# A recurrent layer in a new order: remainders on VectorE, gelu-branch tiles between the gate groups and through DRAM, and a fixed order of the last products

## Chip, cores and metric

The kernel runs on one core of one Trainium2 chip. The metric is the device time in microseconds of one execution. Several executions are timed and their median counts; one execution is profiled, and all rows below come from it.

## What is computed

A decoder trunk of two layers over 1024 tokens of width 1024, in float32. The change touches the mixer of the first layer, the start of both SwiGLU stages, and the final norm:

```python
def rglru_mixer(h, w_in, conv_w, conv_b, w_ra, b_ra, w_ix, b_ix, lam, w_out):
    u = h @ w_in
    xb, yb = u[..., :D_RNN], u[..., D_RNN:]          # D_RNN = 1536
    y = jax.nn.gelu(yb)
    xc = causal_conv4(xb, conv_w) + conv_b
    r = sigmoid(block_diag(xc, w_ra) + b_ra)          # 16 blocks of 96
    i = sigmoid(block_diag(xc, w_ix) + b_ix)
    log_a = -8.0 * r * softplus(-lam)
    a = exp(log_a)
    bx = sqrt(-expm1(2 * log_a)) * (i * xc)
    rec = scan(lambda h, (a, b): a * h + b, a, bx)    # over the tokens
    return (rec * y) @ w_out

h = x + rglru_mixer(rmsnorm(h), ...)
h = h + swiglu(rmsnorm(h), w_gu[0], w_down[0])
h = h + nsa_mixer(rmsnorm(h), shared_kv)
h = h + swiglu(rmsnorm(h), w_gu[1], w_down[1])
return rmsnorm(h) * final_g
```

## The kernel before

Activations lie transposed, channels on the 128 partitions and the 1024 tokens along the row. Every float32 product is done by three matmuls of rounded parts (`mm3`): each operand is split (`split`) into a rounded part, the hi part, copied by ScalarE, and the remainder, the lo part, which is the operand less its hi part, on VectorE or, with `pool=True`, on GpSimd. There are 49 SBUF slots of 128x1024 and 8 PSUM banks of 128x512; a tile gets a slot when an earlier one has been read for the last time. A scheduler sets each engine's order from modelled durations, except where a `manual_schedule` block keeps the order of the program: in `rglru` that holds for ScalarE, VectorE and SyncE until `man.close()`.

**Recurrent layer** (`rglru`). w_in gives 12 x tiles and 12 y tiles of 128 channels, 48 matmuls of 128x512 each. An x tile is evicted from PSUM with the norm's row factor rb (tile xb, L390), convolved on ScalarE and in three VectorE steps (xc, L396), and split into ch and cl; its last 32 partitions go by DMA into the tiles c3h and c3l, as the 16 blocks of 96 channels lie across tiles (`chain`). Every three x tiles have one gate group (`gates`): 16 PSUM tiles pg (48 matmuls), a sigmoid of each on ScalarE (tiles ra and ix, L424), and six DMAs that bring the last 32 partitions back. The group's elementwise work (`ew`) then follows in four steps spread over the next tiles as the table `EW` says: tanh, exp and square root on ScalarE (t, e, s), on VectorE ix times xc (m, L446) and per tile one r step: v (L451), times v (L452) and the scan over the tokens (L453), whose result goes to DRAM (rec, L455). A y tile is evicted (y, L496 or L510), kept in SBUF, and at the end put through gelu, multiplied by the reloaded rec (recl) and split into zh and zl, with which the product with w_out begins (po). TensorE's order before is x0 x1 x2 x3 x4 y0 g0 x5 x6 x7 y1 g1 x8 x9 x10 y2 g2 x11 y3 y4 y5 g3 y6 y7 and then, outside the manual block, y8 to y11.

The weights are loaded ahead and split in the order of their use by `wpump`; the splits numbered 4 to 21 (`WPOOL`) have their remainder on GpSimd, as has every cl.

**FFN stages**, each cut into products numbered i. While the first run, the row factor of the norm is made: sums (pms), a root (`rstd_a`, on VectorE with one power on GpSimd) giving two diagonal tiles dg (L298), and four matmuls prb (L310, `rstd_b`) that spread it over the partitions, after product i = 6.

**Tail.** The last product of the down projection (pU, then pW in two halves of 256 tokens) is added to h; sums of squares of the finished columns run on ScalarE, VectorE and GpSimd; `finish` makes root, dg (L288), prb (L1086) and 16 or 8 output multiplications (out, L1092) for one part of the tokens: 512, then 256, then 256, each sent to DRAM from SyncE or ScalarE.

Of the kernel before, what the change touches and what calls it, by code (L numbers as in the profile page):

```python
# [7 lines left out]
F32 = mybir.dt.float32  # L8
# [5 lines left out]
P = 128  # L14
# [16 lines left out]
GATE_T = [4, 7, 10]  # L31
EW = "t e m0,s m1 m2 r0,r1 r2"
WPOOL = (4, 22)
# [12 lines left out]
XA = 3  # L46

# [20 lines left out]
class Trunk:  # L68
# [44 lines left out]
    def weights(self):  # L113
        d = self.d
        w = []
        def gate_w(g):
            w.append((f"ra{g}", d["w_ra"][g], 384))
            w.append((f"ix{g}", d["w_ix"][g], 384))

        for t in range(DRNN_T):  # L120
            w.append((f"x{t}", d["w_in"][t], 1024))
            if t in GATE_T:
                g = GATE_T.index(t)
                w.append((f"y{g}", d["w_in"][12 + g], 1024))
                gate_w(g)
        for t in range(3, DRNN_T):
            w.append((f"y{t}", d["w_in"][12 + t], 1024))
            if t == 5:
                gate_w(3)
# [73 lines left out]
    def wpump_(self, nload, nsplit):  # L203
# [12 lines left out]
        while self.wsplit < min(nsplit, cap):  # L216
# [8 lines left out]
            self.split(hi[:r, :n], lo[:r, :n], raw[:r, :n], WPOOL[0] <= self.wsplit < WPOOL[1])  # L225
# [44 lines left out]
    def rstd_a(self, ss, nb=KD):  # L270
# [43 lines left out]
    def rglru(self):  # L314
# [72 lines left out]
        def chain(t):  # L387
# [12 lines left out]
            self.split(hi, lo, xc, True)  # L400
# [4 lines left out]
            for a, b in zip(st["x3"], (hi, lo)):  # L405
                nc.sync.dma_start(a[32 * j:32 * j + 32, :].bitcast(F32), b[96:128, :].bitcast(F32))
# [3 lines left out]
        def gates(g, mid=()):  # L410
# [3 lines left out]
            for nme, dst, cb in (("ra", rr, C_BRA), ("ix", ii, C_BIX)):  # L414
                whi, wlo = self.wget(f"{nme}{g}")
# [13 lines left out]
                for b in range(3):  # L429
                    nc.sync.dma_start(dst[b][96:128, :], o[32 * b:32 * b + 32, :])  # L430
# [17 lines left out]

            def scan(b):
                t = 3 * g + b  # L450
                nc.vector.scalar_tensor_tensor(vv[b], rr[b], 1.0, vv[b], op0=ALU.add, op1=ALU.mult)  # L451
                nc.vector.tensor_tensor(ii[b], ii[b], vv[b], ALU.mult)  # L452
# [6 lines left out]
            for b in range(3):  # L459
                fs[f"m{b}"] = lambda b=b: mul(b)  # L460
                fs[f"r{b}"] = lambda b=b: scan(b)
# [16 lines left out]
        def yload(t):  # L478
            if t < DRNN_T:
                recs[t] = self.slot("recl")  # L480
                nc.gpsimd.dma_start(recs[t], st[("rec", t)])
# [1501 lines left out]
```

## Time and profile before

| | |
|---|---|
| runs | 2738.09, 2741.74, 2742.91 us; median 2741.74 |
| the profiled execution | 2742.32 us, span 2740.6 us, mean granted TensorE clock 0.988 |
| busy: TensorE, VectorE, ScalarE, GpSimd | 97%, 69%, 47%, 41% of the span |
| recurrent layer up to the first po | 0 to 346.4 us |
| FFN stage 0 begins, FFN stage 1 begins | 477 us, 2067 us |

Times in the rows are microseconds from the start of the span unless marked ns. In a timeline a row gives start, duration, engine, program line, operation, output from inputs, shape, and in brackets the idle time of the engine just before it with what ended it. L followed by a number is a line of the kernel before.

### The profile page before, as it was taken

How to read it: one execution, taken by the hardware profiler on the slowest of the kernel's cores; microseconds unless marked ns; L12 is line 12 of the kernel's file. 1: busy time of each engine (PE TensorE's matmuls, PEld its weight loads, DVE VectorE, ACT ScalarE, POOL GpSimd, SP SyncE). 2: the span in 40 equal slices, each digit the busy share in tenths (PEclk: the TensorE clock that was granted, in tenths of full speed). 3: DMA queues.
4: the chain of work that ended last, by engine and by line, in shares of the span. 5: the costliest groups of instructions: out<-in, count | busy, mean ns of one | idle time of the engine just before them, and what ended most of it. 6: DMA issues, size and time to landing. Idle time of an engine off the chain costs nothing.

```text
span 2740.6 us, 36687 instructions
## 1 busy us (share of the span) xinstructions
PE 2658.2 (97%) x12650; PEld 2204.7 (80%) x12650; DVE 1892.1 (69%) x3641; ACT 1301.7 (47%) x2505; POOL 1120.5 (41%) x1102
## 2 busy tenths in 40 slices
PE   8989999999999999999999999999999999999997
PEld 6867888788888778888888878888887888887786
DVE  8655734755555898647647999999856545557997
ACT  4656622433223443424415888989934323223433
POOL 2431103444333555110004677777634434436552
PEclk9998999999999999999999999999999999999998
DMA  3323533466564975353485322221354666559761
GB/s 126 93 83 104 170 143 111 112 156 166 150 161 117 324 201 112 133 154 91 162 244 155 82 67 59 67 76 49 108 174 104 170 156 152 154 128 287 194 146 62
DMA packets 175178, 377.03 MB, mean 138 GB/s; under 512 B 16896, under 2 KB 66432, under 8 KB 174992
## 3 DMA queue, kind: packets, MB, share of 16 engines
q1 hardware_dynamic: 121232, 256.79, 28.8%
q0 software_dynamic: 51872, 115.43, 19.6%
q10 hardware_dynamic: 1888, 2.46, 0.2%
q8 instruction: 100, 1.64, 0.2%
q14 instruction: 86, 0.70, 0.1%
HBM read 289.68 MB, written 78.64 MB: 134 GB/s over the span
## 4 chain that ended last, share of the span: by engine, by line
PE 68%; DVE 13%; issue 4%; DMA 3%; ACT 2%; POOL 1%; POOLq 0%; DVEq 0%; SPq 0%; ACTq 0%
PE pb L777 13%; PE pc L777 8%; PE pa L777 8%; PE pn L239 7%; PE pU L1022 6%; PE psc L239 4%; PE po L239 4%; DVE so L232 3%; PE pt L1644 2%; PE py L239 2%; PE pV L1022 2%; PE pwo L1834 2%; PE pW L1022 1%; PE po L1682 1%; PE po L1683 1%
## 5 line engine op out<-in xcount | busy, mean ns | idle before, releaser
L232 DVE TENSOR_TENSOR so<-wr,so 128x512 fp32r<-128x512 f32 (+1 forms) x476 | 390.9, 851 | 55.2 <-ACT so L231 54.6
L231 ACT ACTIVATE so<-wr 128x512 fp32r<-128x512 f32 (+1 forms) x476 | 279.1, 611 | 247.1 <-DMA wr<-w_dn 114.3
L777 PE MATMUL pb<-so,so 128*128 128x512 f32 x1584 | 382.8, 392 | 0.7 <-DVE so L232 0.7
L777 PEld LDWEIGHTS pb<-so,so 128*128 128x128 f32 x1584 | 300.2, 190 | 63.6 <-DVE so L232 1.1
L777 PE MATMUL pa<-so,so 128*128 128x512 f32 x1056 | 254.2, 393 | 4.1 <-ACT ev L786 2.6
L777 PE MATMUL pc<-so,so 128*128 128x512 f32 x1056 | 255.6, 389 | 0.0
L190 POOL DMA_DIRECT2D wr<-w_gu x176 | 161.6, 1076 | 226.0 <-DVE so L232 178.9
L1022 PE MATMUL pU<-so,so 128*128 128x512 f32 x1056 | 245.4, 390 | 2.3 <-DVE so L232 2.3
L777 PEld LDWEIGHTS pa<-so,so 128*128 128x128 f32 x1056 | 199.5, 189 | 46.6 <-DVE so L232 2.7
L239 PE MATMUL psc<-kl,ql 96*128 96x512 f32 (+2 forms) x960 | 232.8, 368 | 2.1 <-DVE thl L232 1.2
L1022 PEld LDWEIGHTS pU<-so,so 128*128 128x128 f32 x1056 | 197.9, 188 | 45.3 <-DVE so L232 4.0
L777 PEld LDWEIGHTS pc<-so,so 128*128 128x128 f32 x1056 | 198.3, 188 | 41.1
L805 ACT ACTIVATE ev<-ev 128x512 f32<-128x512 f32 x44 | 27.8, 632 | 349.4 <-POOL ev L804 349.4
L239 PEld LDWEIGHTS psc<-kl,ql 96*128 96x128 f32 x960 | 164.1, 190 | 24.7 <-PE pt L1644 2.2
L190 POOL DMA_DIRECT2D wr<-w_dn x96 | 91.4, 1136 | 135.7 <-DVE so L232 46.1
L804 POOL TENSOR_TENSOR ev<-ev,rb 128x512 f32<-128x512 f32 x44 | 58.2, 1322 | 209.0 <-DVE ev L803 209.0
L232 DVE TENSOR_TENSOR wl<-wr,wh 128x1024 fp32r<-128x1024 f32 (+4 forms) x79 | 87.8, 1127 | 77.5 <-ACT wh L231 53.2
L232 DVE TENSOR_TENSOR thl<-pt,thl 128x512 fp32r<-128x512 f32 x198 | 133.0, 681 | 10.3 <-ACT thl L231 10.1
L1022 PE MATMUL pV<-so,so 128*128 128x512 f32 x528 | 125.0, 392 | 8.6 <-DVE so L232 6.0
L231 ACT ACTIVATE wh<-wr 128x1024 fp32r<-128x1024 f32 (+4 forms) x97 | 90.1, 956 | 77.6 <-DMA wr<-w_q 19.7
L1022 PEld LDWEIGHTS pV<-so,so 128*128 128x128 f32 x528 | 98.2, 188 | 33.4 <-DVE so L232 7.7
L231 ACT ACTIVATE thl<-pt 128x512 fp32r<-128x512 f32 x198 | 114.5, 597 | 20.2 <-PE pt L1644 18.8
(331 smaller groups left out, 6366.7 us busy)
## 6 DMA issues: line engine op xcount, KB each, us to landing
wr<-w_gu SPq DMA_DIRECT2D x110, 512.0 KB, 4.8
wr<-w_gu POOLq DMA_DIRECT2D x176, 256.0 KB, 5.1
zd<-ev SPq DMA_DIRECT2D x44, 512.0 KB, 3.2
zr<-zd SPq DMA_DIRECT2D x44, 512.0 KB, 6.3
wr<-w_dn SPq DMA_DIRECT2D x40, 512.0 KB, 7.2
wr<-w_dn POOLq DMA_DIRECT2D x64, 256.0 KB, 5.1
ql<-qd SPq DMA_DIRECT2D x64, 192.0 KB, 3.1
wr<-w_in SPq DMA_DIRECT2D x23, 512.0 KB, 3.8
```

The costliest lines, as they stand in the source:

```text
L190: self.nc.gpsimd.dma_start(dst, src, accum_op=ALU.add)
L231: nc.scalar.activation(hi, src, AF.Copy)
L232: (nc.gpsimd if pool else nc.vector).tensor_tensor(lo, src, hi.bitcast(F32), ALU.subtract)
L239: self.nc.tensor.matmul(ps, a, b, start=j == 0, stop=j == n - 1)
L777: nc.tensor.matmul(p, a, b, start=k + n == 0 and j in (1, 5, 6), stop=k == 3 and n == 2, skip_group_check=j not in (1, 5, 6))
L804: nc.gpsimd.tensor_tensor(t0[:, hi], t0[:, hi], rb[:, hi], ALU.mult)
L805: nc.scalar.activation(t0[:, hi], t0[:, hi], AF.Silu)
L1022: nc.tensor.matmul(ps, a, b, start=k + n == 0 and j in (1, 5, 2), stop=k == G[g] - 1 and n == 2, skip_group_check=j not in (1, 5, 2))
L1644: nc.tensor.transpose(pt[:, h * P:(h + 1) * P], Pt[n][h][r][:, off:off + P], self.ident)
L1682: nc.tensor.matmul(po[n], v, thl[:, 0:512], start=False, stop=False)
L1683: nc.tensor.matmul(po[n], v, thl[:, 512:1024], start=False, stop=end)
L1834: self.nc.tensor.matmul(p, wk[a], x[b], start=k + j == 0, stop=k == KD - 1 and j == 2)
```

## The change

**Recurrent layer.** The table `RG` gives one order of x tiles, y tiles and gate groups (g): TensorE now runs x0 x1 x2 y0 x3 x4 y1 g0 x5 x6 y2 x7 g1 x8 y3 x9 x10 y4 g2 x11 y5 y6 g3 y7 y8 and then y9 y10 y11. All remainders are VectorE's. A group's weights are one 768-wide tile. The small moves (c3h, c3l, ra, ix) go to GpSimd's DMA queue. The elementwise work is cut finer (a: L451 of before, b: L452, c: the scan) and all of it is issued before the next gates. Every y tile is stored to DRAM after its eviction and loaded again with rec, two tiles ahead of its use; gelu, product and split of a z follow each other.

**FFN stages.** The four prb matmuls come after product i = 7 and ahead of i = 8; two pairs of small operations of the root are one each.

**Tail.** The remainders for the last product are made earlier; the order of TensorE, VectorE, ScalarE and GpSimd from the last product on is written out (`tail`): 24 pW matmuls ahead of prb, the first quarter's root beside the second quarter's products, tiles 4 to 7 scaled by ScalarE and multiplied by GpSimd, output in smaller pieces.

```diff
-GATE_T = [4, 7, 10]
-EW = "t e m0,s m1 m2 r0,r1 r2"
-WPOOL = (4, 22)
+RG = "y0 x3 x4 y1 g0 x5 x6 y2 x7 g1 x8 y3 x9 x10 y4 g2 x11 y5 y6 g3 y7 y8"
+EW = "t e m0 s m1 m2 a0 b0,c0 a1 b1 c1,a2 b2,c2"
...
-            self.split(hi[:r, :n], lo[:r, :n], raw[:r, :n], WPOOL[0] <= self.wsplit < WPOOL[1])
+            self.split(hi[:r, :n], lo[:r, :n], raw[:r, :n])
...
-        nc.vector.tensor_tensor(t, y, y, ALU.mult)
+        nc.vector.scalar_tensor_tensor(t, y, -0.5, y, op0=ALU.mult, op1=ALU.mult)
         nc.vector.tensor_tensor(t, t, v, ALU.mult)
-        nc.vector.tensor_scalar(t, t, -0.5, 1.5, op0=ALU.mult, op1=ALU.add)
-        nc.vector.tensor_tensor(rt, y, t, ALU.mult)
+        nc.vector.scalar_tensor_tensor(rt, t, 1.5, y, op0=ALU.add, op1=ALU.mult)
...
-            self.split(hi, lo, xc, True)
+            self.split(hi, lo, xc)
...
-                nc.sync.dma_start(a[32 * j:32 * j + 32, :].bitcast(F32), b[96:128, :].bitcast(F32))
+                nc.gpsimd.dma_start(a[32 * j:32 * j + 32, :].bitcast(F32), b[96:128, :].bitcast(F32))
...
-                    nc.sync.dma_start(dst[b][96:128, :], o[32 * b:32 * b + 32, :])
+                    nc.gpsimd.dma_start(dst[b][96:128, :], o[32 * b:32 * b + 32, :])
...
+        def yev(t, pp):
+            y = self.slot("y")
+            for p, c0 in zip(pp, (0, 512)):
+                nc.vector.tensor_tensor(y[:, c0:c0 + 512], p, st["rb"][:, c0:c0 + 512], ALU.mult)
+            dr = st[("y", t)] = self.dram(f"y{t}", [P, S])
+            nc.gpsimd.dma_start(dr, y)
             yield
+        def yload(t):
+            if t < DRNN_T:
+                recs[t] = self.slot("recl"), self.slot("yl")
+                nc.gpsimd.dma_start(recs[t][0], st[("rec", t)])
+                nc.gpsimd.dma_start(recs[t][1], st[("y", t)])
+        def z(t):
+            yload(t + 2)
+            r, y = recs.pop(t)
+            nc.scalar.activation(y, y, AF.Gelu_apprx_tanh)
+            nc.vector.tensor_tensor(y, y, r, ALU.mult)
+            hi, lo = self.slot("zh", F32R), self.slot("zl", F32R)
+            self.split(hi, lo, y)
+            zs[t] = (hi, lo)
...
+        for x in RG.split():
+            i = int(x[1:])
+            if x[0] == "g":
+                while st.get("ew"):
+                    run(ew())
+                gates(i, pend)
+                pend = iter(())
+                continue
...
-            if i == 6:
+            if i == 8:
                 st["rb"] = self.rstd_b(dg)
...
+                if (j, p) == (4, 3):
+                    with self.tc.manual_schedule(engines={getattr(mybir.EngineType, x) for x in TMS.split()}):
+                        self.tail(h, pr, fin, st, scale)
...
+        for p in range(4):
+            next(pr)
+            square(0, p)
...
+        dg = root(sums(0), side)
+        add(1, 2)
+        next(pr)
+        square(1, 3)
+        spread(0, dg)
+        for m in (4, 7, 0):
+            part(0, m)
+        dg = root(sums(1), lambda: part(0, 1))
+        for m in (5, 6, 2, 3):
+            part(0, m)
+        send(0, 4, 4, nc.sync)
+        send(0, 0, 4, nc.sync)
+        spread(1, dg)
+        for m in (4, 0, 5, 1, 6, 2, 3, 7):
+            part(1, m)
```

VectorE ahead of the third gate group (g2), before. ix, v and ra are the second group's elementwise tiles, xb and xc the x tiles 9 and 10:

```order
L453 SCALAR_TENSOR_TENSOR ix_1132<-ra_1071,ix_1132 128x1024
L396 SCALAR_TENSOR_TENSOR xc_1382<-xb_1379,cv,xc_1382 128x1023
L396 SCALAR_TENSOR_TENSOR xc_1382<-xb_1379,cv,xc_1382 128x1022
L396 SCALAR_TENSOR_TENSOR xc_1382<-xb_1379,cv,xc_1382 128x1021
L451 SCALAR_TENSOR_TENSOR v_1179<-ra_1087,v_1179 128x1024
L452 TENSOR_TENSOR ix_1152<-ix_1152,v_1179 128x1024
L453 SCALAR_TENSOR_TENSOR ix_1152<-ra_1087,ix_1152 128x1024
L390 TENSOR_TENSOR xb_1489<-px_1329,rb_386 128x512
```

VectorE ahead of the same group, in the changed kernel (x tiles 9 and 10, then y4; wl and cl are remainders):

```order
L452 SCALAR_TENSOR_TENSOR ix_1206<-ra_1150,ix_1206 128x1024
L390 SCALAR_TENSOR_TENSOR xc_1505<-xb_1502,cv,xc_1505 128x1023
L227 TENSOR_TENSOR cl_1514<-xc_1505,ch_1513 128x1024
L227 TENSOR_TENSOR wl_1525<-wr_1383,wh_1524 128x1024
L384 TENSOR_TENSOR xb_1578<-px_1452,rb_386 128x512
L390 SCALAR_TENSOR_TENSOR xc_1581<-xb_1578,cv,xc_1581 128x1023
L227 TENSOR_TENSOR cl_1587<-xc_1581,ch_1586 128x1024
L227 TENSOR_TENSOR wl_1595<-wr_1446,wh_1594 128x1024
L489 TENSOR_TENSOR y_1620<-py_1528,rb_386 128x512
```

The group's last scan (ix_1206) stood directly ahead of the eviction of x10 that frees banks for the gates (ix_1152 ahead of xb_1489); now it stands ahead of x9's convolution, with x10's eviction and chain and y4's eviction behind it, and the remainders cl and wl are rows of VectorE.

GpSimd around the second gate group, before (remainders among the stores of rec):

```order
L232 TENSOR_TENSOR cl_905<-xc_895,ch_904 128x1024
L232 TENSOR_TENSOR wl_919<-wr_773,wh_918 128x384
L455 DMA rec_914<-ix_714 128x1024
L455 DMA rec_980<-ix_725 128x1024
L232 TENSOR_TENSOR cl_991<-xc_975,ch_990 128x1024
L455 DMA rec_988<-ix_745 128x1024
L232 TENSOR_TENSOR wl_1001<-wr_836,wh_1000 128x1024
```

and in the changed kernel:

```order
L454 DMA rec_963<-ix_781 128x1024
L400 DMA c3h_648<-ch_969 32x1024
L400 DMA c3l_649<-cl_970 32x1024
L454 DMA rec_977<-ix_792 128x1024
L491 DMA y_1112<-y_1109 128x1024
L454 DMA rec_1115<-ix_803 128x1024
L425 DMA ra_1123<-ra_1161 32x1024
L425 DMA ra_1134<-ra_1161 32x1024
```

GpSimd has no arithmetic left there, and its queue holds the stores of rec and y and the small moves, each behind the ones above it.

TensorE at the start of the first FFN stage, before (pb_3454 and pb_3498 are the banks of products 6 and 7, then 8 and 9):

```order
L777 MATMUL pb_3454<-so_3297,so_3300 128x512 x3
L310 MATMUL prb_3468<-dg_3416,onesr 128x512
L310 MATMUL prb_3472<-dg_3416,onesr 128x512
L777 MATMUL pb_3498<-so_3285,so_3317 128x512 x3
L777 MATMUL pb_3498<-so_3289,so_3317 128x512 x3
L310 MATMUL prb_3468<-dg_3418,onesr 128x512
L310 MATMUL prb_3472<-dg_3418,onesr 128x512
L777 MATMUL pb_3454<-so_3363,so_3346 128x512 x3
```

and in the changed kernel:

```order
L740 MATMUL pb_3509<-so_3316,so_3344 128x512 x3
L740 MATMUL pb_3509<-so_3320,so_3344 128x512 x3
L740 MATMUL pb_3509<-so_3324,so_3344 128x512 x3
L304 MATMUL prb_3540<-dg_3442,onesr 128x512
L304 MATMUL prb_3544<-dg_3442,onesr 128x512
L304 MATMUL prb_3540<-dg_3444,onesr 128x512
L304 MATMUL prb_3544<-dg_3444,onesr 128x512
L740 MATMUL pb_3480<-so_3390,so_3373 128x512 x3
```

The twelve matmuls of the next product, which stood between the two pairs of prb, now stand ahead of all four.

## Rows read from the trace of the kernel before

**Rows 1.** The page, busy time, share of the span and instructions of TensorE:

```profile
PE 2658.2 (97%) x12650; PEld 2204.7 (80%) x12650; DVE 1892.1 (69%) x3641; ACT 1301.7 (47%) x2505; POOL 1120.5 (41%) x1102
```

**Rows 2.** Windows of the four gate groups: busy by engine, then PEclk, DMA share, GB/s:

```profile
82.31:93.69 11.38, 11.35 (x49) 7.71 (x48) 6.40 (x7) 10.42 (x16) 5.15 (x3) 1.00 0.42 127
137.26:154.91 17.65, 14.48 (x49) 9.21 (x48) 10.16 (x8) 12.65 (x19) 10.41 (x6) 0.81 0.42 131
198.48:220.68 22.20, 13.98 (x50) 9.12 (x48) 15.23 (x11) 13.34 (x18) 8.58 (x4) 0.77 0.38 122
264.25:281.09 16.84, 14.44 (x49) 9.58 (x48) 11.27 (x11) 14.16 (x19) 1.06 (x2) 0.80 0.38 120
```

**Rows 3.** Waits of TensorE, 0 to 350 us: total, times, longest:

```profile
PE pg L239 <- ACT ra L424: 11.0, 3, 8.2
```

**Rows 4.** Timeline of the third gate group, 194 to 214 us, four engines:

```profile
209.65 0.74 PE L239 MATMUL pg<-ch,wh 96*96 96x512 f32 x1 [8.22 <-ACT ra L424]
...
207.61 1.28 ACT L424 ACT_TABLE_LOAD   x1 [3.76 <-DVE ix L453]
...
194.69 2.29 DVE L453 TENSOR_TENSOR_SCAN ix<-ra,ix 128x1024 f32<-128x1024 f32 x1
...
203.22 4.32 DVE L453 TENSOR_TENSOR_SCAN ix<-ra,ix 128x1024 f32<-128x1024 f32 x1
...
202.05 3.34 POOL L232 TENSOR_TENSOR cl<-xc,ch 128x1024 fp32r<-128x1024 f32 x1 [4.24 <-ACT ch L231]
```

**Rows 5.** Groups of GpSimd, 0 to 350 us: busy us, mean ns:

```profile
L232 POOL TENSOR_TENSOR cl<-xc,ch 128x1024 fp32r<-128x1024 f32 x12 | 33.4, 2780 | 91.3 <-ACT ch L231 91.3
L232 POOL TENSOR_TENSOR wl<-wr,wh 128x1024 fp32r<-128x1024 f32 x12 | 32.0, 2680 | 43.7 <-ACT wh L231 43.6
```

**Rows 6.** Groups of VectorE, 0 to 360 us:

```profile
L453 DVE TENSOR_TENSOR_SCAN ix<-ra,ix 128x1024 f32<-128x1024 f32 x12 | 31.6, 2633 | 0.3
...
L396 DVE SCALAR_TENSOR_TENSOR xc<-xb,cv,xc 128x1023 f32<-128x1023 f32 x12 | 16.0, 1336 | 23.0 <-ACT xc L393 22.8
...
L390 DVE TENSOR_TENSOR xb<-px,rb 128x512 f32<-128x512 f32 x24 | 15.3, 682 | 30.5 <-POOL wl L232 11.6 <-PE py L239 5.4 <-DMA rec<-ix 5.2
...
L232 DVE TENSOR_TENSOR wl<-wr,wh 128x1024 fp32r<-128x1024 f32 x11 | 13.3, 1220 | 22.0 <-ACT wh L231 22.0
```

**Rows 7.** DMA issues, 0 to 350 us: count, KB each, median us to landing:

```profile
wr<-w_in SPq DMA_DIRECT2D x23, 512.0 KB, 3.8
rec<-ix POOLq DMA_DIRECT2D x12, 512.0 KB, 3.0
recl<-rec POOLq DMA_DIRECT2D x12, 512.0 KB, 4.1
...
c3h<-ch SPq DMA_DIRECT2D x12, 128.0 KB, 2.3
```

**Rows 8.** Window 300 to 350 us, columns as in rows 2:

```profile
300.00:350.00 50.00, 50.00 (x222) 41.42 (x221) 49.44 (x46) 21.82 (x23) 10.66 (x20) 1.00 0.56 194
```

**Rows 9.** Timeline of TensorE, start of FFN stages 0 and 1:

```profile
508.30 1.12 PE L310 MATMUL prb<-dg,onesr 128*128 128x512 f32 x2 [2.89 <-DVE dg L298]
...
513.67 5.63 PE L777 MATMUL pb<-so,so 128*128 128x512 f32 x24
...
2092.92 1.22 PE L310 MATMUL prb<-dg,onesr 128*128 128x512 f32 x2 [3.97 <-DVE dg L298]
2093.94 5.29 PE L777 MATMUL pb<-so,so 128*128 128x512 f32 x12
```

**Rows 10.** Timeline of the tail, TensorE and VectorE:

```profile
2706.25 1.74 PE L1086 MATMUL prb<-dg,ones 128*128 128x512 f32 x2 [1.89 <-DVE dg L288]
2707.00 13.50 PE L1022 MATMUL pW<-so,so 128*128 128x256 f32 x96
...
2725.19 1.22 PE L1086 MATMUL prb<-dg,ones 128*128 128x256 f32 x2 [2.29 <-DVE dg L288]
...
2730.26 6.35 DVE L1092 SCALAR_TENSOR_TENSOR out<-h,cv,prb 128x256 f32<-128x256 f32 x16
```

More of the change, by code (lines that the diff above doesn't have):

```diff
@@ L46 @@
 XA = 3
+TMS = "PE DVE Activation Pool"
 C_G = 0
@@ L116, in gate_w, with f @@
         def gate_w(g):
[L117 to L129, printed above, removed]
+            def f(t):
+                for a, x in ((0, d["w_ra"]), (384, d["w_ix"])):
+                    self.nc.sync.dma_start(t[:, a:a + 384], x[g])
+            return f
+        for x in ["x0", "x1", "x2"] + RG.split() + ["y9", "y10", "y11"]:
+            i = int(x[1:])
+            w.append((x, gate_w(i), 768) if x[0] == "g" else (x, d["w_in"][i if x[0] == "x" else 12 + i], 1024))
         for m in range(KD):
@@ L459, in gates @@
             for b in range(3):
-                fs[f"m{b}"] = lambda b=b: mul(b)
-                fs[f"r{b}"] = lambda b=b: scan(b)
+                for x, f in (("m", mul), ("a", sa), ("b", sb), ("c", scan)):
+                    fs[f"{x}{b}"] = lambda b=b, f=f: f(b)
             st["ew"] = [[fs[x] for x in y.split()] for y in EW.split(",")]
@@ L919, in down @@
-        if last:
-            next(fin)
-            next(fin)
-            f1 = self.finish(h, st.pop(256), 256, 256)
-            with self.tc.high_priority(offset=PRIO):
-                next(f1)
-            for f in (fin, f1):
-                for _ in f:
-                    pass
-            yield h
-        else:
-            yield kv
+                if j == 4:
+                    next(fin)
+                    scale(p + 4, hi)
+                if (j, p) == (4, 3):
+                    with self.tc.manual_schedule(engines={getattr(mybir.EngineType, x) for x in TMS.split()}):
+                        self.tail(h, pr, fin, st, scale)
@@ L963, in xop @@
             X.setdefault((g, j), []).append(t)
+            if j == 4:
+                raw[g][k] = None
             if j == order[6]:
-                raw[g][k] = raw[g][G[g] + k] = None
+                raw[g][G[g] + k] = None
         def prep(i):
@@ L1059, in block_proj @@
             hget(i + 4)
-            pump(i)
             o = order.index(j)
+            if tail and (g, o) == (len(G) - 1, 5):
+                pump(i + 2)
+                if p == 0:
+                    for k in range(G[g]):
+                        xop(g, order[6], k)
+            else:
+                pump(i)
             if tail and i >= len(seq) - 4:
@@ L1067, in block_proj @@
             ng, nj = (g, order[o + 1]) if o < 6 else (g + 1, order[0])
-            if ng < len(G) and p < G[ng]:
+            if ng < len(G) and p < G[ng] and not (tail and (g, o) == (len(G) - 1, 5)):
                 xop(ng, nj, p)
@@ L1082, in finish @@
         dg, _ = self.rstd_a(ss, wd // P)
-        yield
-        yield
+        for _ in range(5):
+            yield
         pb = self.ps("prb")[:, 0:wd]
```

218 lines of the change are left out of this document (117 added, 101 removed).

## The prediction

> **What bounds the kernel now.** I read the busy shares first. TensorE is busy 97% of the span [rows 1], so the kernel is bound by its matmuls wherever none is late, and a change that leaves their number alone can only give back time in which TensorE waits, or runs at its lower clock after a wait. The change leaves the number alone, so I looked for such places in the stretches that it touches: the recurrent layer, the start of the two FFN stages, the last 40 us.
>
> In the recurrent layer the windows of the four gate groups are the view that counts [rows 2]. Each holds 48 matmuls. At full clock (granted 1.00, the 2.4 GHz level) the first window takes 11.38 us; the other three take 17.65, 22.20 and 16.84 us at mean granted clocks of 0.81, 0.77 and 0.80. Against 11.38 each they lose 6.3 + 10.8 + 5.5 = 22.6 us. The waits say on whom: 11.0 us in three waits on the sigmoid, the longest 8.2 [rows 3]. The timeline of the third group shows the chain behind the longest [rows 4]: the matmul at 209.65 waits 8.22 us for a free bank, ScalarE's table load at 207.61 waits for a scan (L453) of the group before, and that scan, started at 203.22 in VectorE's fixed order, takes 4.32 us where the scan at 194.69 takes 2.29, because GpSimd's remainder cl ran from 202.05 for 3.34 us. So two things are late there: old elementwise work that stands ahead of the gates, and VectorE held up while GpSimd works. The clock falls after each such gap, and that is the other half of the 22.6 us.
>
> **The recurrent layer, step by step.** *Removed from GpSimd:* 24 remainders of 128x1024, 33.4 + 32.0 us [rows 5], and six of the gate weights. VectorE takes them at 1.22 us each (its own wl row) and the gate weights as one remainder of 768 columns per group, three quarters of that or 0.92 us [rows 6]: 24 x 1.22 + 4 x 0.92 = 33 us more for VectorE. *Given back to VectorE:* the stretching. The scan's mean is 2.63 us [rows 6] against 2.29 undisturbed [rows 4]: 12 x 0.34 = 4 us; the other operations with two SBUF inputs are stretched too, which I put between 4 and 14 us in all (a third to one time GpSimd's single stretches of 2 us as at 203.22, of which there are about a dozen). So VectorE has some 20 to 29 us more to do. *Does it fit?* Between two gate groups the new order has, at most crowded, x5 x6 y2 x7 and the group itself, 5 x 11 = 55 us of TensorE. VectorE needs there 3 x (1.22 + 1.36 + 4.0 + 1.22) for the x tiles (weight remainder, two evictions of 0.682, three convolution steps of 1.34, cl), 2.6 for the y tile, 0.92, and 9 x 1.22 + 3 x 2.29 = 17.9 for the group's elementwise work: 45 us, 82%. It fits, and what decides is the order: by the rows quoted ahead, the last scan of the second group now stands two tiles of TensorE's work ahead of the third gates and no longer just in front of them; for the second gates it still ends about when they begin. Replaying the three late groups with these durations, I find the sigmoid 1 to 2 us late at most in each, so of the 22.6 us I leave 3 standing. **Gates: -19.5 us**, between -22.6 and, if each late group keeps half its loss, -11.
>
> *Moved to GpSimd's queue:* 24 moves of c3h/c3l and 24 of ra/ix, each waiting for its producer, with the stores of y and rec queued behind. One by SyncE lands in 2.3 us, a four times larger rec store on GpSimd's queue in 3.0 [rows 7]; the price is between -0.2 and +0.7 us per move, and as the three moves of a gate tensor go out one behind another, up to 2 us ahead of the first tanh. Nothing but the group's own elementwise work stands behind it, which has 40 us: 0. That queue under a saturated VectorE can be read off the stretch 300 to 350, where VectorE is busy 49.44 of 50 us [rows 8]: its recl loads land in 4.1 us, SyncE's equally large weights in 3.8 [rows 7]. The Trainium skill ("SBUF — State Buffer", the box on VectorE blocking DMAs, in the section on SBUF's two sides) says that GpSimd cannot write a DMA's descriptors while VectorE holds the port pair in a 2-port operation, and names 620 ns that became 3100; that rule speaks against this change. This trace's two rows differ by 0.3 us, so it does not bite here; by the rule's ratio each of three moves in a chain would land some 2.5 us later (an estimate from that page), the gates' gain would be nearer 15, and the sum 4 us higher.
>
> *Added:* 12 stores and 12 loads of y, 12.6 MB. In 300 to 350 the DMA engines moved 194 GB/s at a share of 0.56, so about 346 GB/s when full: 1.5 us per 512 KB tile. After the last gates TensorE has five y tiles, 55 us, and then the first products of w_out, which by their order need the last z's some 22 us in: 77 us. VectorE has 17.9 (group 3), 13 (five y tiles with weights), 12 x 2.44 (product and remainder of z) = 29 and 4 for w_out: 64. The DMA has 24 loads, 36 us, after about 30 us. Both end before 77, with some 7 us to spare: 0, at the other end +8. Before, this stretch cost nothing either (TensorE busy all 50 us).
>
> **FFN starts.** In both stages prb waits for dg, 2.89 and 3.97 us, with twelve ready matmuls (pb of the next product) behind it in the program; in the second stage these then ran at half clock, 5.29 us [rows 9]. Now they stand ahead of prb and fill 2.8 us of the wait (24 such took 5.63 at full clock). The first product behind prb still needs an eviction that is queued behind dg on VectorE, so not all is gained: **-2.5 and -2.5 us**, between -1 and -9 together.
>
> **Tail.** prb waits 1.89 us and the 96 products behind it start at 2707.00, take 13.50 with a half-clock start, and end at 2720.50; at full clock they are 96 halves of 0.235, 11.3 [rows 9, 10]. With 24 of them ahead of prb neither wait nor slow start is left, though five more remainders stand ahead of the root on VectorE (3 us): the products end about 2717.5, -3. After them comes the chain sum, root, dg, prb twice, then 16 output multiplications in 6.35 us from 2730.26, and the span ends at 2740.6. Now the first quarter's root and outputs lie ahead of or beside the last products, so one root remains: from 2717.5 the same chain (4.7 us from 2720.50 to its prb at 2725.19) gives 2722.2, then four leftover and five own multiplications on VectorE at 0.40 and three on GpSimd (a quarter of cl's 2.78 us, 0.7 each, beside it): 2725.8. The last transfers: 4.0 us as before (2736.6 to 2740.6), but 2 MB now leave within 4 us, some 6 us at 346 GB/s: end about 2730.5. **Tail: -10 us**, between -5 and -13.
>
> **Sum.** -19.5 - 5 - 10 = -34.5 on the profiled execution of 2742.32: 2707.8, call it **2708**. The median of the runs is 2741.74, 0.6 us less, which I leave inside the rounding. 0.2% (5.5 us) is about what a measurement of this kernel can tell from no change.
>
> **Rivals.** (a) *The gates stall on.* VectorE is 82% loaded in the crowded stretch, and ScalarE's sigmoids stand in a fixed order behind hi-parts whose producers are on VectorE; half the loss stays. For: VectorE really has 20 us more. Against: the removed scans in front of the gates. The gain is 11 + 5 + 10: 2716. (b) *The last z's are late.* 7 us of margin in 77, shared by VectorE and 12 MB more; a wait of 8 us with the half clock behind it: 2708 + 8 to 10 = 2717. (c) *Slower:* the reloads of rec and y go through GpSimd's queue one behind another, each at its full landing time of 4.1 us [rows 7], not overlapped: 24 x 4.1 = 98 us from 30 us after the last gates on, 133 with the last z's work against a cover of 77: 56 us of waiting, 34.5 gained, 2764. It decides from (77 - 30 - 5)/24 = 1.75 us per load on, and the change is lost from (77 + 34.5 - 35)/24 = 3.2 us on. Against: 194 GB/s were moved there already, more than one tile in flight. By the skill's rule named above, starved descriptors would lead to this same case. (d) *The tail gives nothing*, as GpSimd's multiplications hold up VectorE's, as cl did the scan: 2708 + 7 = 2715.
>
> **Chances.** Forecast (2700 to 2714) 0.55; (a) 0.14; (b) 0.16; (d) 0.08; (c) 0.04; all others, among them both (a) and (b) near no change, 0.03. The range from 2697 (every term at its better end gives 2697.7) to 2723 (a and d together) holds 8 in 10. Faster by over 0.2%: 0.93; within: 0.03; slower: 0.04, rival (c) alone.
>
> **What would show it.** Right: the four gate windows near 11 to 13 us at a granted clock near 1.0; pg's waits on the sigmoid under 3 us in all; no GpSimd arithmetic in the first 350 us and the scan's mean at 2.3; the first po without a wait behind y11; prb's waits in the FFN stages under 1.5 us; one root behind the last product and an end some 13 us after it. Wrong: waits of pg of 5 us or more (a); po waiting for a zl (b, c), with recl and yl landing in over 4 us; L938 stretched beyond 0.6 us (d).

## The result, and the profile after

The changed kernel takes 2708.64 us (median of four runs, 2704.66 to 2712.12) against 2740.9 us before (four runs, 2738.09 to 2742.91): a ratio of 0.9883, 95% interval 0.9865 to 0.9900. The medians differ by 32.3 us. The profiled execution has a span of 2705.8 us, 34.8 less than before; the forecast was 2708 us, 34.5 less than the profiled execution before. The total came out; its parts did not, and the rest of this text is on them.

TensorE's row of the page says how little else there is to give, as in [rows 1]:

```profile
PE 2650.6 (98%) x12658; PEld 2202.0 (81%) x12658; DVE 1893.1 (70%) x3650; ACT 1299.8 (48%) x2504; POOL 1090.7 (40%) x1152
```

The four gate groups, in the same view as [rows 2] (span of the window, then busy time by engine, PEclk, DMA share, GB/s):

```profile
91.33:102.43 11.10, 11.10 (x50) 7.77 (x49) 3.48 (x4) 8.64 (x14) 3.00 (x6) 1.00 0.27 82
145.97:157.06 11.09, 11.09 (x49) 7.77 (x48) 7.66 (x7) 9.51 (x15) 2.18 (x5) 1.00 0.31 112
211.48:222.57 11.09, 11.09 (x49) 7.77 (x48) 3.65 (x4) 9.67 (x15) 2.97 (x6) 1.00 0.27 81
255.23:267.12 11.89, 11.36 (x50) 7.69 (x48) 7.41 (x7) 10.10 (x15) 3.08 (x6) 1.00 0.63 214
```

All four run at a granted clock of 1.00, three without any gap, the last with one of 0.5 us. TensorE's waits up to 340 us, answering [rows 3], hold no sigmoid any more:

```profile
PE px L374 <- ACT xh L247: 6.0, 1, 6.0
PE px L374 <- DVE xl L248: 0.7, 1, 0.7
PE pg L234 <- DVE y L489: 0.5, 1, 0.5
```

The kernel before had two more waits in that stretch, which the prediction did not read. Both are gone:

```profile
PE pg L239 <- DVE xb L390: 2.8, 1, 2.8
PE pms L274 <- DVE ss L266: 2.0, 1, 2.0
```

VectorE's groups for 0 to 350 us, answering [rows 6], show that the stretching is gone (busy us, mean ns): the scan takes 2.29 us in the mean and no longer 2.63, the sums of squares ahead of the first root (ss) 1.22 where they took 1.51 before (second block).

```profile
L452 DVE TENSOR_TENSOR_SCAN ix<-ra,ix 128x1024 f32<-128x1024 f32 x12 | 27.4, 2286 | 0.2
...
L227 DVE TENSOR_TENSOR cl<-xc,ch 128x1024 fp32r<-128x1024 f32 x12 | 14.7, 1226 | 10.3 <-ACT ch L226 10.0
...
L261 DVE TENSOR_TENSOR ss<-ss,sq 128x1024 f32<-128x1024 f32 x7 | 8.6, 1224 | 0.6
```

```profile
L266 DVE TENSOR_TENSOR ss<-ss,sq 128x1024 f32<-128x1024 f32 x7 | 10.6, 1510 | 0.6
```

Since much code in between is the same, I cut each profile at five TensorE events (from timelines: the first po; the first pa of FFN stage 0; the first pU behind it; the same two of stage 1; the end of the last pU) and compare stretches in us. A difference in a stretch that an edit does not touch is what one profile scatters by.

| kernel | median | to first po | po to stage 0 | stage 0 | between | stage 1 | to last pU | tail |
|---|---|---|---|---|---|---|---|---|
| before | 2740.9 | 346.39 | 130.6 | 428.4 | 1161.2 | 424.6 | 213.2 | 36.2 |
| changed | 2708.6 | 321.56 | 130.6 | 424.6 | 1163.2 | 422.6 | 213.7 | 29.6 |
| changed, again | 2707.6 | 321.97 | 130.7 | 424.9 | 1163.9 | 424.2 | 213.3 | 29.6 |
| remainders on GpSimd | 2714.6 | 327.74 | 132.1 | 424.5 | 1163.7 | 423.0 | 213.6 | 29.5 |
| before, remainders on VectorE | 2729.3 | 336.56 | 130.6 | 427.1 | 1160.2 | 422.8 | 212.3 | 35.8 |
| moves on SyncE | 2704.5 | 320.81 | 130.6 | 425.1 | 1159.2 | 423.5 | 213.8 | 29.5 |
| prb after i = 6 | 2709.0 | 320.15 | 132.2 | 425.6 | 1160.4 | 424.4 | 212.3 | 29.5 |
| old tail | 2711.0 | 320.04 | 130.6 | 424.2 | 1162.5 | 423.2 | 212.5 | 34.5 |
| tail, addition sooner | 2707.0 | 321.97 | 130.8 | 425.4 | 1163.1 | 423.5 | 212.6 | 29.4 |
| root with priority | 2708.3 | 320.59 | 131.3 | 425.1 | 1162.1 | 423.6 | 212.9 | 29.6 |
| y9 to y11 kept | 2705.8 | 320.32 | 130.6 | 424.7 | 1162.9 | 423.2 | 212.8 | 30.0 |
| coarse EW | 2715.1 | 329.19 | 131.8 | 424.9 | 1160.5 | 422.7 | 214.9 | 29.9 |
| moves on SyncE, y kept | 2704.8 | 320.70 | 130.6 | 425.8 | 1163.2 | 422.3 | 212.0 | 29.6 |
| first transfers left out (one run) | 2705.7 | 320.20 | 130.8 | 424.5 | 1161.8 | 425.0 | 212.5 | 29.2 |

The stretch between the stages, which no edit touches, scatters over 4.7 us, and the stretch to the first po by 1.9 in the seven profiles that leave it alone (320.04 to 321.97). Where an edit leaves them alone, stage 0 takes 424.2 to 425.8, stage 1 422.3 to 425.0 and the changed tail 29.5 to 30.0. So of the 34.8 us, 24.8 came from the recurrent layer (24 to 26 with that scatter), 3.8 and 2.0 from the FFN stages and 6.6 from the tail, and 2.5 went back in stretches of unchanged code, which says nothing. Of the FFN stages only stage 0 shows a gain clear of scatter: the two profiles with the old code there took 428.4 and 427.1. In stage 1 they took 424.6 and 422.8, no longer than the new code.

### The profile page after: what moved, and what is told of

It is laid out like the page before. It is cut to its first block, busy times and chain, and to the rows that moved or that the text cites. A ratio compares the mean times of both kernels' runs of the same rounds, so it can differ in the third digit from the quotient of the medians.

```text
span 2705.8 us, 36709 instructions
## 1 busy us (share of the span) xinstructions
PE 2650.6 (98%) x12658; PEld 2202.0 (81%) x12658; DVE 1893.1 (70%) x3650; ACT 1299.8 (48%) x2504; POOL 1090.7 (40%) x1152
## 4 chain that ended last, share of the span: by engine, by line
PE 70%; DVE 10%; issue 4%; DMA 2%; ACT 2%; POOL 2%; POOLq 0%; DVEq 0%; SPq 0%; ACTq 0%
PE pb L740 12%; PE pc L740 8%; PE pa L740 8%; PE pn L234 7%; PE pU L1077 6%; PE psc L234 4%; PE po L234 4%; PE pwo L1900 3%; PE pV L1077 3%; PE pt L1710 3%; DVE so L227 2%; PE py L234 2%; PE pW L1077 2%; DMA wr<-w_dn 1%; PE po L1748 1%
## 5 line engine op out<-in xcount | busy, mean ns | idle before, releaser
L227 DVE TENSOR_TENSOR wl<-wr,wh 128x1024 fp32r<-128x1024 f32 (+4 forms) x93 | 105.0, 1143 | 73.0 <-ACT wh L226 61.3
```

The lines of the kernel that those rows point to most:

```text
L227: (nc.gpsimd if pool else nc.vector).tensor_tensor(lo, src, hi.bitcast(F32), ALU.subtract)
```

## The experiments

**The remainders or the order?** First the changed kernel with the remainders on GpSimd:

```diff
-            self.split(hi, lo, xc)
+            self.split(hi, lo, xc, True)
-            self.split(hi[:r, :n], lo[:r, :n], raw[:r, :n])
+            self.split(hi[:r, :n], lo[:r, :n], raw[:r, :n], 4 <= self.wsplit < 22)
```

> The changed kernel with the remainders of the 18 weight tiles and of the 12 ch/cl pairs back on GpSimd; the new order stays. Profile of the changed kernel: first po at 321.56 us, no gap in any gate group; before: 346.39. Theory (both are needed: GpSimd's remainders hold VectorE up, and the new order only keeps old scans away from the gates): the scan's mean is again over 2.5 us, pg waits come back for 3 to 10 us in all with half-clock stretches behind them, first po at 326 to 336, the whole 5 to 14 us slower than the changed kernel. Rival, the order alone: first po within 2 us of 321.6, no wait of pg over 1 us. Rival, the remainders alone: first po at 340 or later.

Measured: 2714.64 us, first po at 327.74, 6.2 later than in the changed kernel, so the theory holds for both. pg waits 3.1 us in all, and the sums of squares cost 2.2 us again. The waits 0 to 350 us and the scan's group show both:

```profile
PE pms L270 <- DVE ss L262: 2.2, 1, 2.2
PE pg L235 <- DVE y L490: 1.6, 2, 1.1
PE pg L235 <- ACT ra L420: 1.5, 1, 1.5
```

```profile
L453 DVE TENSOR_TENSOR_SCAN ix<-ra,ix 128x1024 f32<-128x1024 f32 x12 | 36.0, 2997 | 0.2
```

The scan is even slower than before (3.00 us against 2.63), yet the gate windows keep a granted clock of 1.00, against the expected half-clock stretches; the longest gap in them is 1.5 us. Then the kernel before, with them on VectorE:

```diff
-WPOOL = (4, 22)
+WPOOL = (0, 0)
-            self.split(hi, lo, xc, True)
+            self.split(hi, lo, xc)
```

> The kernel before with all remainders on VectorE and nothing else changed. Theory (both are needed): the scan runs at 2.3 us, but the last scan of a group still stands ahead of the next gates and VectorE has 20 us more to do, so only part of the loss goes: first po at 332 to 342 against 346.39, waits of pg on the sigmoid 4 to 9 us against 11.0; 5 to 14 us faster than before. Rival, the remainders alone: first po at 325 or earlier. Rival, the order alone: first po at 344 or later, or later than before as VectorE is fuller.

Measured: 2729.33 us, first po at 336.56, 9.8 us earlier than before; the scan is back at 2.29 us. pg's waits on the sigmoid are 7.6 us, the longest 5.8, and the third and fourth windows still run at 0.83 and 0.79. The second, which took 17.65 us at 0.81 before, now takes 13.08 at 1.00. The second and third window:

```profile
135.05:148.13 13.08, 11.84 (x49) 7.55 (x48) 11.00 (x10) 10.38 (x16) 0.53 (x1) 1.00 0.50 160
191.70:211.39 19.69, 13.84 (x49) 9.11 (x48) 16.24 (x14) 13.73 (x19) 0.53 (x1) 0.83 0.44 137
```

The two groups lost their time in different ways. In the third the table load still waits for the old scan, which is no longer stretched but still stands there (compare 207.61 in [rows 4]):

```profile
198.46 1.28 ACT L424 ACT_TABLE_LOAD   x1 [1.75 <-DVE ix L453]
```

In the second group of the kernel before, TensorE's longest gap was not for a sigmoid: it waited for an eviction, and VectorE, ahead of that eviction, for GpSimd's remainder wl:

```profile
144.35 1.29 DVE L390 TENSOR_TENSOR xb<-px,rb 128x512 f32<-128x512 f32 x2 [3.26 <-POOL wl L232]
145.09 0.47 PE L239 MATMUL pg<-c3h,wh 96*96 96x512 f32 x1 [2.81 <-DVE xb L390]
```

So the remainders are worth 9.8 us in the old order, and the rest of the change to the recurrent layer is worth 18.7 us with the old remainders; 28.5 if they added up and 24.8 together. That rest is more than the order: with it came the finer cut, the way of the y tiles through DRAM, with their gelu behind the last gates, the queue of the small moves and the wider gate weights. Of these only the cut and the queue are taken apart below. Both parts are needed to lose nearly all gaps; the rest is the larger.

**How finely the elementwise work is cut.** The new order with a coarser table:

```diff
-EW = "t e m0 s m1 m2 a0 b0,c0 a1 b1 c1,a2 b2,c2"
+EW = "t e m0,s m1 m2,a0 b0 c0 a1 b1 c1,a2 b2 c2"
```

> The changed kernel with the elementwise work of a group in three steps and no longer in four cut finer (tanh, exp, first product; root and other products; then whole tiles of v, product and scan, two and one), the order of x tiles, y tiles and gates unchanged. Theory (what frees the gates is that a whole tile of TensorE's work and all elementwise work stand between, not how finely it is cut): first po within 1.5 us of 321.6, waits of pg under 2 us. Rival, the fine cut matters, as an eviction or a convolution behind a run of two scans comes late: waits of pg 2 to 8 us, first po 3 to 10 us later.

Measured: 2715.06 us, first po at 329.19, 7.6 later than in the changed kernel; pg waits 4.0 us in all. The theory fell, the rival holds: with two whole tiles of v, product and scan in one step, x10's convolution ends 3.3 us later, ScalarE's ch and wh with it, and the table load for the sigmoids comes 4.2 us into the third group (216.62, group from 212.44 on) where it comes 1.8 into it in the changed kernel (213.29, group from 211.48 on). ScalarE's timelines, first with the coarse table, then of the changed kernel (start, duration, idle time ahead in brackets):

```profile
214.60 1.06 ACT L226 ACTIVATE ch<-xc 128x1024 fp32r<-128x1024 f32 x1 [4.07 <-DVE xc L390]
215.56 1.04 ACT L226 ACTIVATE wh<-wr 128x1024 fp32r<-128x1024 f32 x1
216.62 1.28 ACT L419 ACT_TABLE_LOAD   x1
```

```profile
211.26 1.06 ACT L226 ACTIVATE ch<-xc 128x1024 fp32r<-128x1024 f32 x1 [4.05 <-DVE xc L390]
212.23 1.04 ACT L226 ACTIVATE wh<-wr 128x1024 fp32r<-128x1024 f32 x1
213.29 1.28 ACT L419 ACT_TABLE_LOAD   x1
```

The first sigmoid starts 1.3 us later each time: 5.5 us into the group with the coarse table, 3.1 in the changed kernel. TensorE gets 18 matmuls far with the free banks (212.44 to 216.77), as its timeline shows:

```profile
216.37 0.40 PE L234 MATMUL pg<-ch,wl 96*96 96x512 f32 x1
218.65 0.48 PE L234 MATMUL pg<-c3h,wh 96*96 96x512 f32 x1 [1.89 <-ACT ra L419]
```

With 0.6 us for one sigmoid (2.41 for four) the changed kernel needs its first bank 4.3 us into the group and has it 3.7 into it: a margin of half a microsecond. With the coarse table the third and fourth groups have one wait of 1.9 us each, the third for a sigmoid, the fourth for the eviction of a y tile, and mean clocks of 0.88 and 0.89.

**The queue of the small moves.** All 48 back on SyncE:

```diff
-                nc.gpsimd.dma_start(a[32 * j:32 * j + 32, :].bitcast(F32), b[96:128, :].bitcast(F32))
+                nc.sync.dma_start(a[32 * j:32 * j + 32, :].bitcast(F32), b[96:128, :].bitcast(F32))
-                    nc.gpsimd.dma_start(dst[b][96:128, :], o[32 * b:32 * b + 32, :])
+                    nc.sync.dma_start(dst[b][96:128, :], o[32 * b:32 * b + 32, :])
```

> The changed kernel with the small moves (c3h, c3l, ra, ix) back on SyncE's queue, where the weight loads are queued in program order. Theory (the queue of the moves is worth nothing either way, since their receivers have slack): first po within 1.5 us of 321.56, the whole within 2 us of the changed kernel. Rival, the move to GpSimd's queue is part of the gain, because on SyncE a move that waits for a sigmoid or a cl holds up the weight loads behind it: waits of px, py or pg for weights, first po 3 to 10 us later. Rival, by the Trainium skill's rule on GpSimd's descriptors (SBUF — State Buffer): the moves land later on GpSimd's queue, so SyncE gives them back sooner and the first tanh of each group comes 1 us or more earlier, with no change in the end.

Measured: 2704.47 us (2701.4 to 2708.33); first po 320.81, which the theory allowed; the whole is 4.2 us lower, which it did not. The moves of ra (KB, median us to landing) are slower on GpSimd's queue than on SyncE's (second line of the two):

```profile
ra<-ra POOLq DMA_DIRECT2D x12, 128.0 KB, 4.3
```

```profile
ra<-ra SPq DMA_DIRECT2D x12, 128.0 KB, 2.3
```

Those of ix land in 2.7 and 2.3 us, c3h in 2.2 either way. A busy VectorE is not what held up ra: in the third group its three moves, issued at 221.1 to 222.1, landed after 4.7 us (median), while VectorE stood idle for 10.05 us up to 226.16. What did stays open.

```profile
ra<-ra POOLq DMA_DIRECT2D x3, 128.0 KB, 4.7
```

```profile
226.16 0.96 DVE L227 TENSOR_TENSOR wl<-wr,wh 128x768 fp32r<-128x768 f32 x1 [10.05 <-ACT wh L226]
```

The gate groups start at the same times in both profiles, and the first tanh of a group comes 0.01, 0.56, 0 and 0.75 us sooner on SyncE, less than the 1 us of the second rival. One step is reached by the queue, the 0.5 us gap of the last group, which every profile with the moves on GpSimd in this order has (or a longer one) and neither of the two with SyncE. A median 4.2 us lower is not explained by that: the profile has 4.0 in the stretch between the stages, which is unchanged code.

**prb after i = 6**:

```diff
-            if i == 8:
+            if i == 6:
                 st["rb"] = self.rstd_b(dg)
```

> The changed kernel with the four matmuls prb again after product i = 6 in both FFN stages. In the changed kernel the first stage (to the first pU of the down projection) is 3.8 us shorter than before, the second 2.0. Theory (the twelve matmuls now fill the wait for dg): prb waits 2.5 to 4 us in each stage again, the two stages together are 3.5 to 6 us longer than in the changed kernel, the whole 2 to 6 us slower. Rival, the shorter root (two operations fewer) and a shorter wait for ev gave most of it: under 1.5 us.

Measured: 2709.03 us, no different. The stages are 1.0 and 1.8 us longer than in the changed kernel's first profile, 2.8 together, which fits neither the theory's 3.5 to 6 nor the rival's 1.5, and both are within the scatter of the table: what this move is worth is not shown. prb waits 1.6 and 3.8 us. In stage 0 that is still less than the 2.89 before, with the twelve matmuls behind it in 2.88 us and not 4.15, and pa waits 1.38 us for ev and not 2.57: so of the 3.8 us gained there the larger part came without this move. The shorter root is the likeliest cause; it was not tested alone. The timeline of stage 1 in the changed kernel tells why little is left (answering [rows 9]):

```profile
2065.39 0.73 PE L304 MATMUL prb<-dg,onesr 128*128 128x512 f32 x2 [1.76 <-DVE dg L292]
2066.52 1.22 PE L304 MATMUL prb<-dg,onesr 128*128 128x512 f32 x2 [0.40 <-DVE dg L292]
2068.41 5.24 PE L740 MATMUL pb<-so,so 128*128 128x512 f32 x12 [0.67 <-DVE ev L754]
```

The twelve matmuls stand ahead of prb, but a wait of 2.2 us in all remains and still costs the clock: the next twelve take 5.24 us, at a granted clock of 0.51.

**The root with priority** in the scheduler:

```diff
-                dg, _ = self.rstd_a(ss)
+                with self.tc.high_priority(offset=PRIO):
+                    dg, _ = self.rstd_a(ss)
```

> The changed kernel with the sums and the root of the FFN norms given priority in the scheduler's order, which puts their first VectorE step seven rows sooner. In the changed kernel prb still waits 0.6 us in stage 0 and 2.2 us in stage 1, where the twelve matmuls behind it then run at half clock (5.24 us against 2.8). Theory (VectorE's order ahead of the root sets the rest of that wait): no wait of prb over 0.5 us, stage 1 to the first pU 2 to 5 us shorter than its 422.6, stage 0 0 to 2 shorter than its 424.6. Rival, the eviction behind dg decides: prb waits less and pb for ev more, both stages within 1 us of the changed kernel. Rival on the slower side: the root's step waits on VectorE for the sums and holds up remainders that TensorE needs, waits of pa or pb for so grow by 1 us or more.

Measured: 2708.27 us; the first rival holds, both stages are within 1 us (425.1 and 423.6). In stage 0 prb no longer waits, but pb's longest wait for so grew from 0.4 to 1.9 us, as the rival on the slower side said. In stage 1 prb waits 1.0 us, and the next product 3.9 instead: it needs the bank pb that the eviction (L754) reads, which the scheduler now puts behind five remainders and one more step:

```profile
2064.43 0.96 PE L304 MATMUL prb<-dg,onesr 128*128 128x512 f32 x3 [0.64 <-DVE dg L292]
2069.33 4.43 PE L740 MATMUL pb<-so,so 128*128 128x512 f32 x12 [3.94 <-ACT rb L305]
```

```profile
2064.89 2.49 DVE L227 TENSOR_TENSOR so<-h,so 128x512 fp32r<-128x512 f32 x4
2067.30 0.68 DVE L227 TENSOR_TENSOR so<-wr,so 128x512 fp32r<-128x512 f32 x1
2067.90 0.68 DVE L677 SCALAR_TENSOR_TENSOR so<-h,so 128x512 fp32r<-128x512 f32 x1
2068.51 0.68 DVE L754 TENSOR_TENSOR ev<-ev,pb 128x512 f32<-128x512 f32 x1
```

The view names ScalarE's rb copy, which ran at 2068.68 beside that eviction; which of the two ended the wait these rows do not part.

**The reloads.** y9 to y11 stay in SBUF, and z takes the tile itself:

```diff
-            dr = st[("y", t)] = self.dram(f"y{t}", [P, S])
-            nc.gpsimd.dma_start(dr, y)
+            if keep:
+                st[("yk", t)] = y
+            else:
+                dr = st[("y", t)] = self.dram(f"y{t}", [P, S])
+                nc.gpsimd.dma_start(dr, y)
```

> The changed kernel with the last three y tiles (y9 to y11) kept in SBUF and not stored and loaded again: 3 of 24 loads and 3 stores fewer between the last gates and w_out, where the reloads landed in 7.7 and 8.4 us (4.1 before) and the DMA engines moved 300 to 410 GB/s. Theory (the reloads are near the limit but hidden): first po at the same time within 0.5 us, loads land sooner (6 to 7 us), no change of the whole beyond 1 us. Rival, the last z's are late in some executions by a few tenths up to 3 us (one run above shows po waiting 1.0 us for zl and zh): the runs are 1 to 3 us faster on the median. Rival on the other side: the three tiles take slots that w_out's weights wait for, po waits for wh or wl, 1 to 4 us slower.

Measured: 2705.82 us, first po at 320.32; recl lands in 6.5 us, yl in 7.1, near the theory's 6 to 7. The whole is 1.8 to 2.8 us below the two medians of the changed kernel, more than the theory's 1 us, and the stretch that the edit reaches is within its scatter. po does not wait in this profile; it waits 1.0 us in all in the run with prb after 6, 0.9 with the remainders on GpSimd, 0.7 with the coarse table, 0.4 with the root's priority, and not at all in the others. With both small edits (moves on SyncE, y kept):

> The changed kernel with both edits that looked a little faster: small moves back on SyncE's queue, y9 to y11 kept in SBUF. Theory (neither was worth anything; their medians of 2704.5 and 2705.8 against 2708.6 came from the stretch between the FFN stages, which they do not touch): first po 320 to 321.5, the whole within 2 us of the changed kernel in the same call. Rival, each is worth 2 to 3 us: 3 to 6 us faster than the changed kernel in the same call, shown in the stretch up to the first po or in that up to FFN stage 0.

> The changed kernel itself once more, beside the others of this call, as the measure for differences of a few microseconds: 2706 to 2711 us. Stages by its first profile: first po 321.56 us, FFN stage 0 424.6, stage 1 422.6, from the first pU of stage 0 to stage 1 1163.2, from the last pU to the end 30.1. In eight profiles of kernels that share the stretch between the FFN stages that stretch took 1159.2 to 1163.7, so one profile's difference of under 5 us there says nothing.

Measured: 2704.80 us (2703.23 to 2705.92) against 2707.64 (2706.11 to 2710.26) for the changed kernel beside it: the four runs of each do not overlap, 2.8 us, between theory and rival. In the table the stretches that the two edits reach differ by no more than they scatter (320.70 to 321.97 up to the first po), and the rest stands in unchanged code, so a gain is likely, on four runs each, and its place is open. It is the fastest version here, beside the moves on SyncE alone.

**The tail.** With the old functions `down`, `block_proj` and `finish`:

> The changed kernel with the down projection's last products, the final norm and the output as they were before; recurrent layer and FFN starts stay changed. In the changed kernel it takes 29.9 us from the end of the last pU to the end of the span (2675.9 to 2705.8), before 36.5 (2704.1 to 2740.6), so theory (the tail is worth what these two stretches differ by): that stretch is 35.5 to 37.5 us again, the whole 5 to 9 us slower than the changed kernel. Rival, the earlier remainders on VectorE cost the stretch before it as much as the tail gives: the whole within 2 us of the changed kernel.

Measured: 2711.03 us, 2.4 above the changed kernel and not 5 to 9; the tail takes 34.5 us, 5.0 more than the changed one and 1.7 less than before. These 1.7 us lie ahead of the products' end: from the end of the last pU to that of the last pW it takes 16.1 us before, 14.4 here and 14.5 in the changed kernel, and prb waits 1.89, 1.07 and 0.97 us. So the written-out order gained nothing up to there, with the shorter root already in; all its 5.0 us lie behind the products (20.1 us before and here, 15.1 in the changed kernel). Then the addition moved ahead of the root's steps:

```diff
             next(pr)
             square(1, 2)
             add(1, 1)
+            next(pr)
+            square(1, 3)
         dg = root(sums(0), side)
         add(1, 2)
-        next(pr)
-        square(1, 3)
         spread(0, dg)
```

> The changed kernel with one step of the written-out tail moved: the last product's second half is added to h and squared ahead of the first quarter's root steps, no longer behind its dg on VectorE. In the changed kernel that product ends at 2690.4, but its addition runs at 2692.16, behind dg, and the last sums wait for it. Theory (that addition is on the path that sets the end): the last prb comes 1.0 to 1.8 us sooner after the last product, the end 0.5 to 1.8 us sooner. Rival, the DMA of 2 MB sets the end: the last prb comes sooner, the span's end does not (within 0.4 us). Second rival: the first quarter's root, now behind the addition, is later by as much and sends later: no change or slower.

Measured: 2706.98 us; the last prb starts 5.4 us after the products' end (2691.7 to 2697.11), without the edit 5.5 (2690.7 to 2696.15), and the tail is 29.4 for 29.6: the second rival. VectorE's rows show the first root late by a sum (L898) that took 1.60 us beside GpSimd's multiplications, and 0.43 at the same place in the changed kernel (second line of each pair the step that begins the root):

```profile
2689.50 1.60 DVE L898 TENSOR_TENSOR ss<-ss,sq 128x256 f32<-128x256 f32 x1 [0.34 <-ACT sq L894]
2691.01 0.15 DVE L910 TENSOR_SCALAR rv<-pms 128x2 f32<-128x2 f32 x1
```

```profile
2688.44 0.43 DVE L898 TENSOR_TENSOR ss<-ss,sq 128x256 f32<-128x256 f32 x1 [0.33 <-ACT sq L894]
2688.78 0.15 DVE L910 TENSOR_SCALAR rv<-pms 128x2 f32<-128x2 f32 x1
```

Whether the move would pay without that stretched sum is not shown.

Last, without the two transfers of the first quarter of the tokens, which then do not reach the output:

```diff
-        send(0, 4, 4, nc.sync)
-        send(0, 0, 4, nc.sync)
```

> The changed kernel without the two transfers that write the first quarter (256 tokens) to DRAM; 1 of the last 2 MB is left out, all arithmetic stays. Theory (the 2 MB that leave within 4 us set the end, about 6 us behind the last multiplication): the last multiplications end as before, the span ends 2 to 3.5 us sooner, 6 to 7.5 us after the last prb and not 9.65. Rival, the chain sets it and each transfer's own latency: the span ends within 0.7 us of 9.65 after the last prb.

Measured in one execution: the span ends 8.9 us after the last prb (2695.10 to 2704.0), not 9.65 (2696.15 to 2705.8). 0.75 us is just beyond the rival's 0.7 and far from the theory's 2 to 3.5. The last transfers, of 256 KB each, land in 2.6 to 2.8 us (median) and not 4.1 to 4.2: the amount of data is the smaller part of the end, the chain and one transfer's latency the larger.

## Why the prediction was right, and where its steps were not

*Gates, -19.5: right mechanism, mis-sized.* Both causes read from [rows 4] were real: the remainders undone alone bring 6.2 us back, everything else undone 15.0. I left 3 us standing for late sigmoids; none stood. And I counted the gates alone: another 2.0 us ahead of them, pms waiting for sums that GpSimd's remainders stretched, went too. The four windows took 68.1 us and take 45.2, 22.9 less; with the 2.0 that is 24.9 for the 24.8. I also read the second group by the third: its gap of 2.81 us was an eviction behind GpSimd's wl, a wait that is not among the 11.0 us of [rows 3]. That the order decided more than the load was said, but without a price.

*Small moves, 0 (between -0.2 and +0.7 per move):* c3h and c3l 0, ra +2.0 us, ix +0.4; the bound was too narrow for ra, since it was taken from single transfers. No stretch shows a cost beyond the 0.5 us gap of the last group, so the term of 0 nearly holds. The Trainium skill's rule on descriptors ("SBUF — State Buffer", the box in the section on its two sides) would have made moves on that queue later while VectorE runs a 2-port operation. The trace does not show it: c3h took 2.2 us on either queue, and the late ra landed late beside an idle VectorE.

*y through DRAM, 0 with 7 us to spare:* no wait in the changed kernel's two profiles, but no margin either: in four other profiles that keep the reloads po waits 0.4 to 1.0 us. recl and yl landed in 7.7 and 8.4 us, one of the signs named for rivals (b) and (c), ScalarE waited 26.7 us for yl, and the last two zl rows end at 343.6 and 344.9, 23 us after the first po, where the forecast put the need for them (22). The step that failed is the DMA work of 66 us, 36 us of loads from 30 us after the gates on. The loads went from 287.3 to 340.1, that is 73 us after the gates. The rate was the forecast one, 346 GB/s, as this window shows (columns as in [rows 2]):

```profile
287.30:340.10 52.80, 52.80 (x234) 43.73 (x234) 40.75 (x38) 23.20 (x23) 19.79 (x38) 1.00 0.93 346
```

What the sum left out are the other transfers of that window: w_out's weights, the layer's input (xT, for the sum h = x + ...) and the last stores of y and rec, some 5.7 of 18.2 MB. Rival (b) came near.

*FFN starts, -5:* 3.8 in stage 0; in stage 1 2.0 by the first profile of the changed kernel and 0.4 by the second, which is not clear of scatter. The term went by the filled wait alone, but the larger part of the 3.8 came without the move of prb, likely by the shorter root. In stage 1 prb still waited 2.2 us (1.5 in the second profile), where under 1.5 was to be the sign of being right; after it came the next wait, an eviction behind dg, as the prediction had said, and half clock.

*Tail, -10: -6.6.* To the end of the products 14.5 us against 16.1, -1.7 of the forecast -3, since prb still waits 0.97 us for dg and the first quarter's sums (pms) now stand among the products. The step that failed behind them is "one root remains behind the last product": the first quarter's root ends there as well. TensorE's rows:

```profile
2680.03 1.12 PE L1147 MATMUL prb<-dg,ones 128*128 128x512 f32 x2 [0.97 <-DVE dg L282]
...
2687.55 3.11 PE L1077 MATMUL pW<-so,so 128*128 128x256 f32 x24
2691.97 0.70 PE L924 MATMUL prb<-dg,ones 128*128 128x256 f32 x2 [1.31 <-DVE dg L918]
...
2696.15 1.22 PE L924 MATMUL prb<-dg,ones 128*128 128x256 f32 x2 [2.24 <-DVE dg L918]
```

The first quarter's prb comes 1.3 us after the products' end at 2690.7, the second 4.2 behind it, 5.5 and not 4.7 after the products; and the end 15.1 us after them, not 13. Of these 2.1 us 0.8 are the second prb's, and 1.2 the end's: it comes 5.9 us behind the last multiplication (2699.9), not 4.7. Rival (d), GpSimd's multiplications holding up VectorE's, did not hold for the outputs: L938 took 0.41 to 0.47 us. It did for one sum, above.

So the gates' mechanism was right, and the total to 0.3 us was luck: an underrated recurrent layer (-5.3) and FFN start (-0.8) nearly cancelled with an overrated tail (+3.4) and 2.5 us in unchanged code.

## What to carry to other kernels

Find the windows in which TensorE's granted clock is below 1, and ask of each which old work stands ahead of the late producer in its engine's fixed order: moving that work a tile earlier, with what else came with the new order, was worth more here (18.7 us) than taking the engine's disturber away (9.8). Read each window's own wait, as two windows that lose alike can do so for different reasons. Price a gain by stages in several profiles, since whole runs scatter by 7 us where the tail scatters by 0.5. And when a wait is filled, look what is queued behind its producer: in the FFN stage and in the tail that was the next wait.

## What the runs showed of the hardware that was not expected

In these runs VectorE is held up beside GpSimd in operations that read both tensors from SBUF (the scan 3.00 us for 2.29 with the remainders on GpSimd), though not in each of them, and not in those that read one from PSUM. In the changed tail four outputs, which read one tensor from SBUF and one from PSUM, take 0.68 us each beside GpSimd's multiplications, no more than the evictions of [rows 6] (xb, 682 ns):

```profile
2684.73 2.72 DVE L1159 SCALAR_TENSOR_TENSOR out<-h,cv,prb 128x512 f32<-128x512 f32 x4
```

```profile
2684.72 5.30 POOL L1157 TENSOR_TENSOR out<-h,rb 128x512 f32<-128x512 f32 x4 [3.47 <-ACT rb L1150]
```

The sum L898, with two tensors in SBUF, took 1.60 us beside such multiplications in the run with the addition moved, and 0.43 beside those above. The Trainium skill says the same of the outputs ("SBUF — State Buffer", section "Who interferes with whom"): an instruction of VectorE with at most one SBUF input, outside the 2-port modes, does not contend with GpSimd. By that rule rival (d), as it stands for the outputs, could have been struck out beforehand.
